# One encoder layer on one core: an earlier start and another order for the steps of the DeltaNet heads, and eight gate units instead of four at the border of two stages

## The chip, the cores and the metric

The kernel runs on one core of one Trainium2 chip. The metric is the device time of the program in microseconds (us). A core has TensorE (PE, with its weight loads as PEld), VectorE (DVE), ScalarE (ACT), GpSimd (POOL) and SyncE (SP), which here issues all DMA transfers from one queue.

## The reference

The layer takes 1024 tokens of width 1024 with 16 learned tokens ahead of them, all in float32. What matters of it:

```
h = rmsnorm(x)
q, k, v, z, b, a, sc_b, sc_c, sc_x, gate_a, gate_b = split(h @ w_in)
o   = gated_deltanet_bidir(q, k, v, z, b, a)      # 8 heads of 128, chunked, forward + backward
y_a = o @ w_branch_dn
y_b = (sc_b * depthwise_conv3(sc_c * sc_x)) @ w_branch_sc
x  += (sigmoid(gate_a) * y_a + sigmoid(gate_b) * y_b) @ w_out
x  += (silu(g) * u) @ w_down                       # g, u = split(rmsnorm(x) @ w_gate_up)
out = rmsnorm(x)[16:]

# one head, one direction, chunk by chunk (S: 128 x 128 state)
v_new = u_c - w_c @ S                              # u, w: solved from a unit triangular matrix
o_c   = (q_c * exp(g)) @ S + qk_c @ v_new
S     = S * exp(g_last) + k_dec_c.T @ v_new
```

q, k and v go through a centred convolution of five taps and SiLU first; q and k are normalised to unit length.

## The kernel before

**Matmuls.** A dense product of float32 is made of three: both operands are split into a high and a low part (a cast on ScalarE, a subtraction on VectorE, `split`, `split_part`), and high*high, high*low and low*high are added up in PSUM.

**The heads' stage.** The projection through w_in is cut into units of 128 output columns: 24 for q, k, v (`u_qkv`), 8 for z (`u_z`), 24 for the short convolution (`u_short`) and 16 for the merge gates (`u_gate`). A unit is two or three row blocks of 24 matmuls each (`dense_steps`, L290). The q, k, v units are taken when `qkv_ok` allows; all others are filling work, in the order z, short convolution, gates. The last LATE = 4 gates are kept back for later.

Beside them run, head by head, four generators: `g_decay` loads a mask-and-decay tile PQ (1 MB, broadcast) and takes its exponential; `g_norm` turns keys and queries with TensorE, squares and sums them, keeps the turned keys in the tile `kn` (two buffers) and multiplies keys and queries chunk by chunk into NP and PQ; `g_inv` inverts the triangular matrices; `g_scan` turns and scales the values (tile `vS`, one buffer) and then walks through eight chunks of 128 tokens from both ends, with four groups of small float32 matmuls per step (L742 and L745, L757, L774, L780) and VectorE and ScalarE between them. After the last step the outputs are normalised, scaled, turned (L83) and multiplied with z, which `g_scan` loads into the tile of the turned keys (L778).

**The inverse.** `g_inv` turns the 32 x 32 diagonal blocks of NP and stores them to DRAM (L591), loads them back as rows (L605), and solves them by substitution on VectorE: 31 pairs of a multiplication and a subtraction (`fs_job`, L446 and L450), each needing the one before. The result goes through DRAM again (L623, L628), and four rounds of small matmuls (L658 to L689) put the blocks together. The inverse's matmuls and the whole of the scan exclude each other through `lock["scan"]`.

**The order of the work** is written by a planner while the program is built. It keeps a model time for each engine (T) and emits a chain's next part when the model says that its inputs are ready; each engine then executes what it was given strictly in that order. VectorE's jobs wait in three lanes, "conv" (the convolutions, L313), "fs" (the substitution) and "norm"; `pump` takes from the ready lane that has spent least, weighted, so a convolution step fills the time in which a substitution step waits for its predecessor (DEP = 127 ns). A row buffer that is needed for a new projection forces the job that still holds it. Four streams hold at most one head each; the norm of head h starts when h < done + 2, where done counts finished scans, the scan when its head is inverted, and a head's projections are picked when h < done + 3. After a unit is picked its weights are loaded, and two units are ahead.

**The border.** After the stage its pools are closed, and the four late gate units follow (`dense`, L119 to L121; weights by `wload`, L104), while the first blocks of the next stage, a product of seven instead of eight block multiplications (`seven`, L1316), are loaded and combined (`front`). Then come the output projection (L1479 to L1481), the gate-up product (L1539 to L1541) and the down product (L1680 to L1682).

Of the kernel before, what the change touches and what calls it, by code (L numbers as in the profile page):

```python
# [8 lines left out]
F32 = mybir.dt.float32  # L9
# [7 lines left out]
P = 128  # L17
# [8 lines left out]
NC = 8  # L26
FF = 2816
NF = FF // P
LATE = 4
EPS = 1e-6  # L30
NEG = -1e30

# [5 lines left out]
def encoder_layer(ctx: ExitStack, tc: tile.TileContext, x, meta, norm1_w, w_in,  # L38
# [16 lines left out]
    def uid(s):  # L55
        cnt["n"] += 1
        return f"{s}_{cnt['n']}"
# [171 lines left out]
    def A(n):  # L229
        return on("act", 144 + 0.834 * n)  # L230
# [37 lines left out]
    def pump():  # L268
        while T["dve"] <= T["pe"] + 700:
            now = max(T["dve"], T["pe"])  # L270
            cand = [k for k, q in lanes.items() if q and q[0].ready <= now + 20]
            if not cand and any(q and q[0].ready <= now + DEP + 20 for q in lanes.values()):
                T["dve"] = now + DEP
                continue
            if not cand:
                return
            k = min(cand, key=lambda q: spent[q])
            spent[k] += lanes[k][0].step() * WEIGHT[k]
            if lanes[k][0].done:
                lanes[k].pop(0)  # L280
# [44 lines left out]
    def u_qkv(h, i, w):  # L325

        st_ = heads[h]
        if i == 0:
            st_["kq"] = d1.tile([P, 2, L], F32, tag="kq", name=uid("kq"), bufs=3)
            st_["vT"] = d1.tile([P, L], F32, tag="vT", name=uid("vT"), bufs=2)  # L330
        col = (8 + h, h, 16 + h)[i]
        dst = (st_["kq"][:, 0], st_["kq"][:, 1], st_["vT"])[i]
        raw = None
        sub = {"rows": 0}
        for ci, (t0, n) in enumerate(QUERY if i == 1 else QCH):
            po = psm()
            yield from dense_steps(po, w, hx, t0, n, sweep=(h == i == ci == 0))
            if raw is None:
                raw = row_buffer()
                if i != 1:  # L340
                    nc.gpsimd.memset(raw[:, 0:2], 0.0)
                nc.gpsimd.memset(raw[:, L + 2:L + 4], 0.0)
            nc.scalar.copy(raw[:, 2 + t0:2 + t0 + n], po[:, :n])
            nc.scalar.activation(dst[:, t0:t0 + n], po[:, :n], AF.Copy, scale=wc[:, 2, col:col + 1])  # L344
            A(n)
            A(n)
            sub["rows"] = 2 + t0 + n if ci < 2 else L + 4
            if ci == 1:
                job = enqueue("conv", conv_job(raw, dst, col, sub, META if i == 1 else 0))
                raws.append(job)  # L350
        key = ("tk", "tq", "tv")[i]

        def watch():
            return job.done
        st_[key] = watch
# [98 lines left out]
    def norm_job(st_, ssk1, cc, ce, he, y, sk):  # L454
        nc.vector.tensor_tensor(out=ce, in0=cc, in1=he, op=ALU.mult)
        V(18)
        yield T["dve"] + DEP
        nc.vector.tensor_tensor(out=sk, in0=y, in1=ssk1, op=ALU.mult)
        V(9)

    lock = {"scan": None}

# [5 lines left out]
    def g_decay(h, st_):  # L468

        st_["exp"] = {}  # L470
        PQ = st_["PQ"] = dn.tile([P, NC, 2, P], F32, tag="PQ", name=uid("PQ"), bufs=2)
        nc.sync.dma_start(PQ, grow[h:h + 1, 0:NC].broadcast_to([P, NC, 2, P]))
        yield T["pe"] + ARRIVE
        for c2 in range(NC // 2):
            pair = PQ[:, 2 * c2:2 * c2 + 2]
            nc.vector.tensor_tensor(out=pair, in0=pair, in1=mask2.unsqueeze(1).broadcast_to([P, 2, 2, P]), op=ALU.add)
            yield V(512)
            for c in (2 * c2, 2 * c2 + 1):
                for d in range(2):
                    hd = d * 8 + h  # L480
                    nc.scalar.activation(PQ[:, c, d], PQ[:, c, d], AF.Exp, bias=negG2[:, c, hd:hd + 1])
                    st_["exp"][c] = on("act", 295)
                yield T["act"]

    def g_norm(h, st_):

        kq = st_["kq"]
        kT, qT = kq[:, 0], kq[:, 1]
        small = dn.tile([P, 9, 12], F32, tag="small", name=uid("small"), bufs=2)
        st_["small"] = small  # L490
        ssk, ssq, rk2, ssk1, y, _, sk = (small[:, :, i] for i in range(7))
        cc, ce = small[:, :, 7:9], small[:, :, 9:11]
        nc.gpsimd.memset(small, 1.0)
        kn = dn.tile([P, 9, P], F32, tag="kn", name=uid("kn"), bufs=2)
        st_["kn"] = kn

        def square(src, dst, p=P):
# [40 lines left out]
                                  start=True, stop=True)  # L538
            return pk, pe(435)

        nxt = kkq(0)
        yield T["act"] + HOP
        nc.vector.tensor_scalar(out=ssk1, in0=ssk, scalar1=EPS, scalar2=None, op0=ALU.add)
        rsqrt(y, ssk1)
# [3 lines left out]
        nc.vector.tensor_tensor(out=cc, in0=hb, in1=rk2.unsqueeze(2).broadcast_to([P, 9, 2]), op=ALU.mult)  # L548
        nc.vector.tensor_scalar(out=Nm, in0=Nm, scalar1=cc[:META, 8, 0:1], scalar2=None, op0=ALU.mult)
        on("dve", 950)  # L550
        NP = dn.tile([P, NC, 2, P], F32, tag="NP", name=uid("NP"), bufs=2)
        PQ = st_["PQ"]
        st_["NP"] = NP
        yield T["act"] + HOP - 300
        for c in range(NC):
            pk, t = nxt
            if c + 1 < NC:
                nxt = kkq(c + 1)
            while c not in st_["exp"]:
# [12 lines left out]

    def g_inv(h, st_):
# [4 lines left out]

        nd = dr.tile([4, NC, 2, 32, 32], F32, tag="nd", name=uid("nd"), bufs=2)
        ndm = dr.tile([META, META], F32, tag="ndm", name=uid("ndm"), bufs=2)  # L580
        fN = dn.tile([P, 32, 32], F32, tag="fN", name=uid("fN"))
        fP = dn.tile([P, 16, 32], F32, tag="fP", name=uid("fP"))
        fPf = fP.rearrange("p j i -> p (j i)")
        mN = dn.tile([P, NC, 32], F32, tag="T2", name=uid("mN")).rearrange("p c i -> p (c i)")[:1]
# [3 lines left out]
        for b in range(4):  # L588
            nc.vector.transpose(NP[B(b), :, 1, B(b)], NP[B(b), :, 1, B(b)])
            on("dve", 467)  # L590
            nc.sync.dma_start(nd[b].rearrange("c d j i -> j (c d) i"),  # L591
                                             NP[B(b), :, :, B(b)].rearrange("j c d i -> j (c d) i"))
            if b < 3:
                yield T["dve"] - 200
        nc.gpsimd.memset(fP, 0.0)
        nc.gpsimd.memset(fPf[0:64, 0:8 * 33:33], 1.0)
        nc.gpsimd.memset(fPf[0:64, 8 * 32 + 24:512:33], 1.0)
# [32 lines left out]
        nc.sync.dma_start(Pm[:META, :META], pdm)  # L630

        Xe = dn.tile([P, NC, 32], F32, tag="Xe", name=uid("Xe"))
        XT = dn.tile([P, 2, 512], F32, tag="XT", name=uid("XT"))
        X64 = XT[:, 0].rearrange("p (c i) -> p c i", c=NC)
        nc.gpsimd.memset(X64[0:32, :, 32:64], 0.0)
        nc.gpsimd.memset(X64[96:128, :, 0:32], 0.0)
# [58 lines left out]
        lock["scan"] = None  # L695

    def g_scan(h, st_):
        nonlocal freed
        kq, vT, small, kn, NP, PQ, Pm = (st_[k] for k in ("kq", "vT", "small", "kn", "NP", "PQ", "Pm"))
        kT, qT = kq[:, 0], kq[:, 1]  # L700
        ssk, ssq, rk2, ssk1, y, _, sk = (small[:, :, i] for i in range(7))
        cc, ce = small[:, :, 7:9], small[:, :, 9:11]
# [7 lines left out]
        for grp in ((8, 0, 7), (1, 2, 3), (4, 5, 6)):  # L710
# [4 lines left out]
            for i, c in enumerate(grp):  # L715
                nc.scalar.activation(vS[:, c], pt[:, i], AF.Copy, scale=sk[:, c:c + 1])
                A(P)
        yield T["act"] + HOP - 1000

        oacc = [NP[:, c, c // 4] for c in range(NC)]  # L720

# [14 lines left out]
        for i in range(NC):  # L736
            cd = (i, NC - 1 - i)
            hd = (h, 8 + h)
            act_ = [d for d in range(2) if S[d] is not None]
            b1, b2 = newbank(), newbank()  # L740
            for d in act_:
                mm(b1[:, d], kT[:, cs(cd[d])], S[d], start=True, stop=True)  # L742
# [6 lines left out]
            for d in act_:  # L749
# [3 lines left out]
                                               op0=ALU.mult, op1=ALU.add)  # L753
                t = V(P, 1)
            yield t
            for d in range(2):
                mm(b1[:, 2 + d], NP[:, cd[d], d], r0[d], start=True, stop=True)  # L757
            yield pe(430)
# [13 lines left out]
            if i < NC - 1:  # L772
                for d in range(2):
                    mm(b1[:, d], kn[:, cd[d]], w[d], start=True, stop=True)  # L774
                t = pe(430)
            if i == NC - 2:
                zT = kn[:, 0:NC]
                nc.sync.dma_start(zT, z_d[h].rearrange("p (c t) -> p c t", c=NC))  # L778
            for d in range(2):
                mm(b2[:, 2 + d], PQ[:, cd[d], d], v2[d], start=True, stop=True)  # L780
            t2 = pe(430)
# [74 lines left out]
    fill_units += [(off + j * P, lambda w, j=j, i=i: u_short(j, i, w), None, i)  # L856
                   for j in range(8) for i, off in enumerate((OSC, OSX, OSB))]
    gates = [(j, off, d_[j]) for off, d_ in ((OGB, tb_d), (OGA, ta_d)) for j in range(8)]
    late = gates[len(gates) - LATE:]
    fill_units += [(off + j * P, lambda w, j=j, d_=d_: u_gate(j, d_, w), None, None) for j, off, d_ in gates[:len(gates) - LATE]]  # L860
    done = freed = 0
    decs, norms, invs, scans = [], [], [], []

    def qkv_ok():
        h, i = qkv_units[0][2:]
        return h < done + 3 and (i < 2 or h < nscan + 2)

    def pick():

# [21 lines left out]
    def start_streams():  # L891
# [3 lines left out]
            decs.append([g_decay(h, heads[h]), T["dve"] + HOP, h])  # L895
            ndec += 1
        h = nnorm
        if h < H and h < ndec and h < done + 2 and not norms and all(k in heads[h] and heads[h][k]() for k in ("tk", "tq")):
            norms.append([g_norm(h, heads[h]), T["dve"] + HOP, h])
            nnorm += 1  # L900
        h = ninv
# [1 line left out]
            invs.append([g_inv(h, heads[h]), T["dve"] + HOP, h])  # L903
            ninv += 1
        h = nscan
        if h < H and not scans and heads[h].get("inverted") and "tv" in heads[h] and heads[h]["tv"]():
            scans.append([g_scan(h, heads[h]), T["dve"] + HOP, h])
            nscan += 1

# [850 lines left out]
```

## Time and profile before

| | |
|---|---|
| median of 3 runs | 1994.02 us (1991.82 to 1994.43) |
| profiled execution | 1993.23 us, span 1991.5 us |
| granted TensorE clock | 0.995 of full, mean |
| instructions | 31817, of them 11977 matmuls |
| busy share | PE 99%, PEld 86%, DVE 71%, ACT 43%, POOL 8% |
| HBM | 184.34 MB read, 68.25 MB written |

The profile is one execution. An engine's line gives the sum of the times in which it was busy. A matmul's length in the records overlaps the next one's; its pace is read from start to start. A stretch's row gives for each engine its busy time and, in brackets, the number of its instructions, then the granted clock, the mean share of the 16 DMA engines and the GB/s. A row of waits gives the waiting engine, line and tile, what it waited for, the total in us, how often, and the longest. A row of the order of time gives start and length in us. "PEld" waiting is TensorE's queue standing before a weight load, which may still lie under a running matmul.

### The profile page before, as it was taken

Reading aid. Unit: us, or ns where it says so; the run is one execution under the profiler, and the core shown is the slowest. Engines: PE = TensorE matmul, PEld = TensorE weight load, DVE = VectorE, ACT = ScalarE, POOL = GpSimd, SP = SyncE. Lnnn points to the kernel's source line nnn. Section 1 sums busy time; section 2 is a strip of 40 time slices with the busy share of each in tenths; the row PEclk is TensorE's granted clock in tenths of the full one; section 3 lists DMA queues with packets and bytes.
Section 4 is the critical chain, followed back from the end, with each engine's and each line's share of the span. In section 5 each row is a group of like instructions: output and inputs, shape, how many; then the busy total and the mean of one; then the engine's idle time right before and its main releaser. Section 6 shows DMA issues by size and latency. Waiting matters only on the chain.

```text
span 1991.5 us, 31817 instructions
## 1 busy us (share of the span) xinstructions
PE 1962.7 (99%) x11977; PEld 1716.6 (86%) x11977; DVE 1406.2 (71%) x2744; ACT 846.6 (43%) x1984; POOL 165.8 (8%) x455
## 2 busy tenths in 40 slices
PE   8899999999999999999999999999999999999998
PEld 8898899999999999988888888787888888888887
DVE  4787476887779697866334888558987777856575
ACT  5364336555536464453442555224322322324343
POOL 3002011212020111201000000000000000000001
PEclk9999999999999999999999999999999999999999
DMA  4124322232322322233327732332765445487654
GB/s 143 42 63 117 104 62 80 65 96 49 96 59 81 75 75 70 65 84 83 106 78 276 259 110 87 111 117 90 262 229 180 157 146 184 156 278 247 194 171 169
DMA packets 245263, 254.66 MB, mean 128 GB/s; under 512 B 46644, under 2 KB 174949, under 8 KB 242677
## 3 DMA queue, kind: packets, MB, share of 16 engines
q1 hardware_dynamic: 245109, 252.63, 40.5%
q8 instruction: 94, 1.54, 0.3%
q14 instruction: 60, 0.49, 0.1%
HBM read 184.34 MB, written 68.25 MB: 127 GB/s over the span
## 4 chain that ended last, share of the span: by engine, by line
PE 92%; DVE 5%; ACT 2%; issue 1%; DMA 1%; SPq 0%; POOLq 0%; POOL 0%; DVEq 0%; ACTq 0%
PE pm L290 37%; PE pd L1541 3%; PE pd L1539 3%; PE pd L1540 3%; PE pm L1539 3%; PE pm L1540 3%; PE pm L1541 3%; PE pd L1316 2%; PE pm L1316 2%; PE pe L1541 2%; PE pe L1539 2%; PE pe L1540 2%; PE pd L757 2%; PE pe L537 1%; PE pe L1316 1%; PE pd L774 1%
## 5 line engine op out<-in xcount | busy, mean ns | idle before, releaser
L290 PE MATMUL pm<-hTh,wh 128*128 128x384 f32 (+4 forms) x1408 | 519.8, 370 | 2.9 <-ACT wh L888 2.8
L290 PE MATMUL pm<-hTh,wl 128*128 128x384 f32 (+4 forms) x1408 | 484.0, 345 | 1.1 <-DVE XT L674 0.9
L290 PE MATMUL pm<-al,wh 128*128 128x384 f32 (+4 forms) x1408 | 482.4, 343 | 0.5 <-DVE al L988 0.5
L290 PEld LDWEIGHTS pm<-hTh,wh 128*128 128x128 f32 x1408 | 266.8, 190 | 20.1 <-ACT wh L888 3.5
L290 PEld LDWEIGHTS pm<-hTh,wl 128*128 128x128 f32 x1408 | 265.4, 189 | 19.8 <-DVE wl L885 0.7
L290 PEld LDWEIGHTS pm<-al,wh 128*128 128x128 f32 x1408 | 266.9, 190 | 15.2 <-DVE al L988 0.7
L87 DVE TENSOR_TENSOR al<-raw,ring_h 128x1024 fp32r<-128x1024 f32 x73 | 88.1, 1222 | 64.5 <-ACT ring_h L86 64.0
L885 DVE TENSOR_TENSOR wl<-raw,wh 128x512 fp32r<-128x512 f32 x132 | 89.4, 689 | 59.0 <-ACT wh L888 58.3
L86 ACT CAST ring_h<-raw 128x1024 fp32r<-128x1024 f32 x73 | 76.5, 1053 | 104.4 <-PE pe L1682 36.2
L313 DVE SCALAR_TENSOR_TENSOR kq<-ra,wc,kq 128x520 f32<-128x520 f32 (+1 forms) x128 | 96.2, 752 | 9.7 <-ACT kq L344 6.6
L764 ACT ACTIVATE w<-pd,small 128x128 f32<-128x128 f32 x128 | 40.0, 364 | 110.6 <-PE pd L757 94.0
L128 POOL TENSOR_SCALAR ss<-ss 128x1 f32<-128x1 f32 x12 | 4.1, 343 | 903.1 <-ACT b L1692 607.8
L888 ACT CAST wh<-raw 128x512 fp32r<-128x512 f32 x132 | 77.0, 617 | 0.1
L450 DVE TENSOR_TENSOR fP<-fP,tm 128x135 f32<-128x135 f32 (+23 forms) x248 | 71.5, 288 | 5.2
L446 DVE TENSOR_TENSOR tm<-fP,fN 128x135 f32<-128x135 f32 (+23 forms) x248 | 71.7, 289 | 4.7
L789 DVE SCALAR_TENSOR_TENSOR S<-S,eGl,pd 128x128 f32<-128x128 f32 x104 | 31.8, 343 | 54.9 <-PE pd L774 26.8
L130 POOL TENSOR_TENSOR small<-small,minus_half 128x9 f32<-128x9 f32 x16 | 29.3, 1832 | 441.0 <-DVE small L824 309.9
L1277 DVE TENSOR_TENSOR b<-pm,b 128x512 f32<-128x512 f32 x65 | 43.6, 685 | 28.9 <-PE pm L1541 26.3
L613 POOL TENSOR_TENSOR tm<-mP,mN 1x15 f32<-1x15 f32 (+7 forms) x120 | 41.7, 347 | 228.4 <-DMA mN<-ndm 219.9
L1277 DVE TENSOR_TENSOR b<-pd,b 128x512 f32<-128x512 f32 x57 | 38.5, 685 | 24.8 <-PE pd L1541 24.7
L86 ACT CAST wh<-raw 128x1024 fp32r<-128x1024 f32 x28 | 29.5, 1053 | 56.7 <-issue 18.5
L313 DVE SCALAR_TENSOR_TENSOR vT<-ra,wc,vT 128x520 f32<-128x520 f32 x64 | 48.2, 753 | 6.4 <-ACT vT L344 5.4
(621 smaller groups left out, 4764.6 us busy)
## 6 DMA issues: line engine op xcount, KB each, us to landing
raw<-in_w_in_dram SPq DMA_DIRECT2D x72, 512.0 KB
raw<-in_w_gate_up_dram SPq DMA_DIRECT2D x44, 512.0 KB
sums<-in_w_down_dram SPq DMA_DIRECT2D x22, 512.0 KB
t_d<-sums SPq DMA_DIRECT2D x11, 1024.0 KB
raw<-s_d SPq DMA_DIRECT2D x44, 256.0 KB
raw<-t_d SPq DMA_DIRECT2D x44, 256.0 KB
act_d<-b SPq DMA_DIRECT2D x43, 256.0 KB
raw<-act_d SPq DMA_DIRECT2D x33, 256.0 KB
```

The source lines that it names most:

```text
L86: nc.scalar.copy(hi, src)
L87: nc.vector.tensor_tensor(out=lo, in0=src, in1=hi.bitcast(F32), op=ALU.subtract)
L290: mm(po[:, :n], (wl if j == 2 else wh)[:, k], xl[k][:, t0:t0 + n] if j == 1 else xh[k][:, t0:t0 + n], start=(i == 0), stop=(i == 3 * KT - 1))
L313: nc.vector.scalar_tensor_tensor(out=acc, in0=raw[:, h0 + t:h0 + t + hn], scalar=wc[:, t, col:col + 1], in1=acc, op0=ALU.mult, op1=ALU.add)
L446: nc.vector.tensor_tensor(out=tv, in0=fP[:, 0:r, j:j + 1].broadcast_to([P, r, n]), in1=fN[:, j:j + 1, j + 1:32].broadcast_to([P, r, n]), o ...
L885: nc.vector.tensor_tensor(out=u[1][1][:, k], in0=u[2][:, k], in1=u[1][0][:, k].bitcast(F32), op=ALU.subtract)
L888: nc.scalar.copy(u[1][0][:, k], u[2][:, k])
L1277: add = lambda out, a, b: nc.vector.tensor_tensor(out=out, in0=a, in1=b, op=ALU.add)
L1316: mm(bank[t], a[:, c], b[:, hi], start=fresh, stop=first and k == 3 and j == 2, skip_group_check=not first)
L1539: mm(po, ah[:, k], bhk, start=k == 0, stop=False)
L1540: mm(po, ah[:, k], blk, start=False, stop=False)
L1541: mm(po, al[:, k], bhk, start=False, stop=k == 3)
```

## The change

- LATE goes from 4 to 8: all eight gates of the DeltaNet branch are made at the border.
- `pump` takes "norm" and "fs" before "conv", and lets VectorE's model time wait for the next substitution step when that is ready within DEP.
- A third buffer of `kn`, four of `small`: the norm of head h may start when h < freed + 3 and any decay has started (freed counts scans whose last products are emitted), and waits ahead of its key products until done >= h - 1 and PQ is there.
- PQ is loaded in four parts, used 4, 6, 8 and 10 us after the request instead of all at 10.
- The scan starts as soon as its norm is finished and its values are convolved: it turns them, gives the lock back, waits for the inverse and takes the lock again. z is loaded into the tile of the turned values, in the last step instead of the one before it.
- Projections of q, k, v are picked when h < near + 3, where near counts scans that have reached their sixth step; `u_qkv` waits for freed >= h - 2.
- The inverse stores its four blocks without pauses between them; its tiles fN and XT share a buffer.

```
-LATE = 4
+LATE = 8
...
+            fs = lanes["fs"]
+            if fs and now + 20 < fs[0].ready <= now + DEP + 20:
+                T["dve"] = now = fs[0].ready
             cand = [k for k, q in lanes.items() if q and q[0].ready <= now + 20]
+            cand = [k for k in ("norm", "fs") if k in cand][:1] or cand
...
         if i == 0:
+            while freed < h - 2:
+                T["pe"] += 100
+                yield
...
-        nc.sync.dma_start(PQ, grow[h:h + 1, 0:NC].broadcast_to([P, NC, 2, P]))
-        yield T["pe"] + ARRIVE
         for c2 in range(NC // 2):
+            nc.sync.dma_start(PQ[:, 2 * c2:2 * c2 + 2], grow[h:h + 1, 2 * c2:2 * c2 + 2].broadcast_to([P, 2, 2, P]))
+        asked = T["pe"]
+        for c2 in range(NC // 2):
+            yield asked + 4000 + 2000 * c2
...
-        kn = dn.tile([P, 9, P], F32, tag="kn", name=uid("kn"), bufs=2)
+        kn = dn.tile([P, 9, P], F32, tag="kn", name=uid("kn"), bufs=3)
...
-        nxt = kkq(0)
...
+        while done < h - 1 or "PQ" not in st_:
+            yield T["pe"] + 100
...
+        nxt = kkq(0)
...
-            if b < 3:
-                yield T["dve"] - 200
...
-        XT = dn.tile([P, 2, 512], F32, tag="XT", name=uid("XT"))
+        XT = dn.tile([P, 2, 512], F32, tag="fN", name=uid("XT"))
...
+        lock["scan"] = None
         yield T["act"] + HOP - 1000
+        while not st_.get("inverted"):
+            yield T["pe"] + 100
+        yield from take("scan")
...
+            near += i == NEAR
...
+            if i == NC - 1:
+                zT = vS[:, 0:NC]
+                nc.sync.dma_start(zT, z_d[h].rearrange("p (c t) -> p c t", c=NC))
...
-            if i == NC - 2:
-                zT = kn[:, 0:NC]
-                nc.sync.dma_start(zT, z_d[h].rearrange("p (c t) -> p c t", c=NC))
...
-        return h < done + 3 and (i < 2 or h < nscan + 2)
+        return h < near + 3 and (i < 2 or h < nscan + 2)
...
-        if h < H and h < ndec and h < done + 2 and not norms and all(k in heads[h] and heads[h][k]() for k in ("tk", "tq")):
+        if h < H and ndec and h < freed + 3 and not norms and all(k in heads[h] and heads[h][k]() for k in ("tk", "tq")):
...
-        if h < H and not scans and heads[h].get("inverted") and "tv" in heads[h] and heads[h]["tv"]():
+        if h < H and not scans and heads[h].get("sk") and "tv" in heads[h] and heads[h]["tv"]():
```

More of the change, by code (lines that the diff above doesn't have):

```diff
@@ L459, in norm_job @@
         V(9)
+        st_["sk"] = True
     lock = {"scan": None}
@@ L488, in g_norm @@
         kT, qT = kq[:, 0], kq[:, 1]
-        small = dn.tile([P, 9, 12], F32, tag="small", name=uid("small"), bufs=2)
+        small = dn.tile([P, 9, 12], F32, tag="small", name=uid("small"), bufs=4)
         st_["small"] = small
@@ L580, in g_inv @@
         ndm = dr.tile([META, META], F32, tag="ndm", name=uid("ndm"), bufs=2)
-        fN = dn.tile([P, 32, 32], F32, tag="fN", name=uid("fN"))
+        fN = dn.tile([P, 2, 512], F32, tag="fN", name=uid("fN")).rearrange("p a (j i) -> p (a j) i", i=32)
         fP = dn.tile([P, 16, 32], F32, tag="fP", name=uid("fP"))
@@ L697, in g_scan @@
     def g_scan(h, st_):
-        nonlocal freed
-        kq, vT, small, kn, NP, PQ, Pm = (st_[k] for k in ("kq", "vT", "small", "kn", "NP", "PQ", "Pm"))
+        nonlocal freed, near
+        kq, vT, small, kn, NP, PQ = (st_[k] for k in ("kq", "vT", "small", "kn", "NP", "PQ"))
         kT, qT = kq[:, 0], kq[:, 1]
@@ L717, in g_scan @@
                 A(P)
+        lock["scan"] = None
         yield T["act"] + HOP - 1000
+        while not st_.get("inverted"):
+            yield T["pe"] + 100
+        yield from take("scan")
+        Pm = st_["Pm"]
         oacc = [NP[:, c, c // 4] for c in range(NC)]
@@ L858, in encoder_layer @@
     gates = [(j, off, d_[j]) for off, d_ in ((OGB, tb_d), (OGA, ta_d)) for j in range(8)]
-    late = gates[len(gates) - LATE:]
+    late = gates[max(0, len(gates) - LATE):]
     fill_units += [(off + j * P, lambda w, j=j, d_=d_: u_gate(j, d_, w), None, None) for j, off, d_ in gates[:len(gates) - LATE]]
-    done = freed = 0
+    NEAR = 5
+    done = freed = near = 0
     decs, norms, invs, scans = [], [], [], []
```

## The prediction

> **What bounds the kernel now.** I read the page first, then busy time by stretch, the waits of TensorE, the order of time around one head and around the border, and the groups of VectorE inside one head's substitution. The page:
>
> ```profile
> span 1991.5 us, 31817 instructions
> PE 1962.7 (99%) x11977; PEld 1716.6 (86%) x11977; DVE 1406.2 (71%) x2744; ACT 846.6 (43%) x1984; POOL 165.8 (8%) x455
> PE   8899999999999999999999999999999999999998
> PEclk9999999999999999999999999999999999999999
> ```
>
> TensorE is busy in every slice, all but 28.8 us of the span. The profiled execution took 1993.2 us, 1.7 more than its span; the median of the runs shown is 1994.0, 0.8 above it. The sum below goes against the 1993.2. Busy time by stretch (columns: PE, PEld, DVE, ACT, POOL, clock, DMA share, GB/s) shows where the 28.8 us lie:
>
> ```profile
> 0.00:50.00 50.00, 44.32 (x305) 41.69 (x306) 22.60 (x37) 26.27 (x54) 18.27 (x46) 1.00 0.47 143
> 50.00:101.00 51.00, 46.00 (x264) 43.22 (x263) 37.49 (x75) 19.50 (x46) 1.79 (x9) 0.90 0.16 42
> 101.00:1053.00 952.00, 948.16 (x7323) 868.89 (x7323) 672.85 (x1783) 464.54 (x1467) 130.46 (x368) 1.00 0.29 80
> 1053.00:1096.00 43.00, 43.00 (x191) 35.60 (x190) 23.33 (x20) 10.04 (x15) 0.00 (x0) 1.00 0.86 305
> 1096.00:1200.00 104.00, 104.00 (x460) 85.97 (x459) 88.87 (x96) 53.06 (x60) 0.00 (x0) 1.00 0.54 183
> 1200.00:1300.00 100.00, 96.13 (x431) 78.29 (x430) 66.74 (x86) 35.42 (x49) 2.40 (x6) 1.00 0.28 90
> ```
>
> The change touches the third row, the stage of the heads, and the fourth, the border with its four gate units. In the heads' stage TensorE is idle 952.00 - 948.16 = 3.8 us of 952; at the border not at all, nor in the hundred us behind it. The first 101 us, with 10.7 us idle, come before the first head has a substitution or a norm, so the planner emits them as before. What is idle after 1200 us belongs to the output projection and later, which the edits do not touch.
>
> That a busy PE is at its pace here, and not merely occupied, is seen in the order of time at the border (start, length):
>
> ```profile
> 1051.21 0.60 PE L83 MATMUL pd<-ident,NP 128*128 128x128 f32 x4
> 1051.56 0.47 PE L290 MATMUL pm<-hTh,wh 128*128 128x512 f32 x1
> 1051.88 0.39 PE L290 MATMUL pm<-al,wh 128*128 128x512 f32 x1
> 1052.10 0.39 PE L290 MATMUL pm<-hTh,wl 128*128 128x512 f32 x1
> 1052.33 0.40 PE L119 MATMUL pm<-hTh,wh 128*128 128x512 f32 x1
> ```
>
> Consecutive 512-column matmuls start 0.22 to 0.23 us apart, on both sides of the border; the fourth row of the stretches says the same (43.00 / 191 = 0.225). Two more things stand here. The last transposes of the last head (L83) come 1 us before the last projection of the stage (L290): chain and filling work now end together. And a gate unit has the same price inside the stage as behind it.
>
> **Gates, four to eight.** A gate unit is 2 x 24 matmuls of 512 columns. Four units are 192 x 0.225 = 43.2 us; they leave the stage and arrive at the border. Net 0: the heads' stage should end near 1053 - 43 = 1010, and the border last 86 us. Their weight loads move with them, each still one of 512 KB on SP, their casts become two long ones, and ScalarE and VectorE are far from full at the border (10.0 and 23.3 us of 43). The loads of the next stage already run there at a DMA share of 0.86 without any wait of TensorE; twice the time makes that easier, not worth more, since there is no wait to remove. I take 0; the bounds are the idle time of the fourth row, none, and a third of a us for each cast that comes late, so 0 to +1.5.
>
> **Substitution first.** The window of head 2's substitution, by groups of VectorE (busy, mean ns), and its first and last instruction:
>
> ```profile
> L313 DVE SCALAR_TENSOR_TENSOR kq<-ra,wc,kq 128x520 f32<-128x520 f32 (+1 forms) x12 | 9.0, 746 | 0.6 <-ACT kq L344 0.4
> L450 DVE TENSOR_TENSOR fP<-fP,tm 128x135 f32<-128x135 f32 (+23 forms) x31 | 8.9, 286 | 0.5
> L313 DVE SCALAR_TENSOR_TENSOR vT<-ra,wc,vT 128x520 f32<-128x520 f32 x8 | 6.0, 746 | 0.0
> L885 DVE TENSOR_TENSOR wl<-raw,wh 128x512 fp32r<-128x512 f32 x8 | 5.5, 683 | 0.0
> L813 DVE TENSOR_TENSOR NP<-pd,NP 128x128 f32<-128x128 f32 x10 | 2.9, 291 | 0.9 <-ACT NP L807 0.6
> L752 DVE SCALAR_TENSOR_TENSOR r<-pd,negEG,vS 128x128 f32<-128x128 f32 x9 | 2.8, 344 | 0.2
> L810 DVE SCALAR_TENSOR_TENSOR NP<-pd,eG,NP 128x128 f32<-128x128 f32 x8 | 2.7, 343 | 0.0
> 368.83 0.18 DVE L446 TENSOR_TENSOR tm<-fP,fN 128x31 f32<-128x31 f32 x1
> 424.01 0.18 DVE L446 TENSOR_TENSOR tm<-fP,fN 128x16 f32<-128x16 f32 x1
> 424.23 0.19 DVE L450 TENSOR_TENSOR fP<-fP,tm 128x16 f32<-128x16 f32 x1
> ```
>
> 62 short dependent steps take 55.6 us. The last pair shows their own pace: 0.22 us from start to start for 0.18 of work, 0.04 over the length. At the mean of 286 ns that is 62 x 0.33 = 20 us. Of the rest, convolution (L313) is 15.0 us, and the edit puts it off; the splits and the scan's steps (5.5 + 2.9 + 2.8 + 2.7 = 13.9 us, a quarter of the window) are not in the lanes and stay between. With the smaller groups I let them fill a third of VectorE's time; then the substitution lasts 20 / 0.67 = 30 us: 25 us less for a head like this one. VectorE gets no more work, only another order, and the idle time that the planner holds for each step's result (its 0.127 us; 62 x 0.127 = 8 us a head, 63 beside the 672.85 of 952 that it is busy). Who may now be late is a convolution, and behind it the projection's row buffer; a planner step forces a waiting convolution through when its buffer is wanted, and TensorE has three banks, 24 x 0.225 = 5.4 us each, before it must stop. Taken at 0; bounds -2 to +4.
>
> **Keys, values, decay.** These shorten one head's path, not the work. How far apart two heads are now, on the SP queue (issues of the first transfer of each inverse, and of the mask's load):
>
> ```profile
> 354.36 3.04 SPq L591 DMA_DIRECT2D nd<-NP  x4
> 398.77 0.34 SPq L472 DMA_DIRECT2D PQ<-grow  x1
> 458.56 2.50 SPq L591 DMA_DIRECT2D nd<-NP  x4
> 508.17 0.34 SPq L778 DMA_DIRECT2D kn<-z_d  x1
> ```
>
> The inverse of head 3 starts 104.2 us after that of head 2. Taking 25 us from it leaves some 80; the values turned beside the inverse take two or three us more off the path, an earlier norm (third key buffer) and the decay in quarters a few us of waiting between heads. The inverse's four stores are emitted without the planner's pauses; SP stands over them for 3.04 us already (first row), with one weight load behind. The z load moves from the seventh step of the scan to the eighth and from the keys' tile to the values', so SP now waits for VectorE's last r instead of a matmul. Its reader and that r:
>
> ```profile
> L752 DVE SCALAR_TENSOR_TENSOR r<-pd,negEG,vS x10: 340/344/350, 485.5 to 510.4; 128x128 f32<-128x128 f32 x10
> 523.22 0.74 DVE L845 SCALAR_TENSOR_TENSOR NP<-pd,cols,kn 128x512 f32<-128x512 f32 x1
> 300.80:304.60 3.80, 3.80 (x25) 3.80 (x25) 3.29 (x11) 0.81 (x4) 0.55 (x1) 1.00 0.82 286
> ```
>
> Issued at about 510.8, it has 12.4 us until its reader; at the 286 GB/s with which the mask's 1 MB moves in the last row, 512 KB take 1.8 us. Hidden; the weight load queued behind it on SP has two units (22 us) of slack. If that cover were gone, VectorE would stand before r and TensorE with it. The mask itself is now four issues of 0.34 us, one more us of SP per head, and VectorE reads the first quarter 4 us after the request instead of 10. By that row a quarter moves in about 1 us, so it is there after 2 us, or 4 with a weight load ahead of it: cost 0 to 1 us a head, taken 0.1, together +1.
>
> **Waits that are added.** A head's projections may be picked from the sixth step of the scan three heads back, and then wait, with nothing emitted but the chains, until that scan's last products. In the r row ten r's, five steps, lie from 485.5 to 510.4: 24.9 / 4 = 6.2 us a step, so under three steps, 17 to 18 us. A picked unit starts two units, 21.6 us, later. Cost 0, with 4 us to spare; without that cover up to 6 us for five heads. The norm now stands before its key products until the scan two heads back is done (behind it only its own stream waits), and the scan between its values and the inverse, its lock returned. The turned values are written on ScalarE after the previous head's last read of the same tile as z; ScalarE's evictions queue behind that write, for at most the 0.74 us of L845.
>
> **What can be won.** Only waits of TensorE. Those of the heads' stage, weight loads included (us in total, times, longest):
>
> ```profile
> PEld pd L757 <- DVE r L752: 3.8, 10, 0.5
> PEld pd L666 <- issue: 3.4, 8, 1.3
> PEld pd L681 <- issue: 2.8, 8, 0.7
> PEld pd L688 <- issue: 2.3, 8, 0.4
> PEld pd L774 <- ACT v L769: 1.9, 10, 0.2
> ```
>
> Together 14.2 us, partly under running matmuls. The middle three come once per head and the inverse's matmuls remain, so I let them stand; the r wait comes from what is ahead of r in VectorE's queue, a 746 ns convolution step or a 683 ns split. With 286 ns substitution steps in the convolution's place I take 1 us off. Sum: 1993.2 + 0 + 0 + 1 - 1 = 1993.
>
> The Trainium skill ("Perfetto Trace Analysis", Identifying the Most-Contended Engine) says that matmul busy time is a bad measure of the room TensorE has left, and to use the busy share of weight loads; by that, 86% would leave 14%. That reading is a rival below; the starts 0.225 us apart are against it.
>
> **Rivals.** (a) Fewer waits: shorter steps ahead of r and inverses that meet fewer long convolution steps. For it: the r row is VectorE's doing. Price: the r row and two thirds of the other four, 5 to 10 us off, 1983 to 1988. 0.25.
>
> (b) TensorE has room after all and the chain is what holds the stage. Price: weight loads are idle 952.00 - 868.89 = 83 us there, so up to that much off, 1910. Against it, the pace at the border, where no head is running, is the same. 0.02. It is the page's rule as a mechanism; here the trace speaks against the rule.
>
> (c) Slower, by VectorE's first-in-first-out queue: the mask's quarter is asked for too early, or a forced convolution sits ahead of r, while a scan runs. The scan's r, and L757 behind it, stand for the difference. It decides when a quarter lands over 4 us after the planner's request, which a busy DMA (0.86 at the border, 0.29 in the stage) would do. Price: 8 heads x 0.7 to 1.5 us, 1999 to 2005. 0.17. A longer wait costs double: around the 5.0 us idle in the second stretch the clock was 0.90 of full, 51 x 0.10 = 5 us more. The Trainium skill ("TensorE: Matmul & The Clock Gate", Part 1) has the same: an idle window of about 3.4 us halves the clock until a busy one has passed; that row agrees.
>
> (d) Slower, because the edit does not shorten the chain: the stage has 43.2 us less filling work, so seven distances between heads must each lose 43.2 / 7 = 6.2 us. Below that TensorE runs dry at the end: +43 at the worst, 2036; at 3 us saved, 2015. Speaking for it: starved convolutions delay the next head's norm. Against: 25 us from the substitution alone. 0.06.
>
> **How the numbers follow.** A change under 0.2% (4 us) is what measurements of this kernel cannot tell from none; the three runs spread by 2.6 us. Forecast 0.50 at 1993, (a) and (b) 0.27 faster, (c) and (d) 0.23 slower. The range 1985 to 2004 holds the forecast, about two thirds of (a) and most of (c): 0.8.
>
> **What would show it.** Right: 11977 matmuls, the last L290 near 1010, the border's stretch 86 us without idle time, substitutions of 27 to 35 us, heads some 80 to 85 us apart, the last head's transposes 50 us or more before the last L290, and idle time of TensorE from 101 us to the border of 2 to 8 us. Wrong: a stretch of only L742 to L780 before the border (d); r or mask waits of VectorE over 1 us (c); matmul starts closer than 0.22 us (b); or a gap or lost clock at the border, which I price at nothing.

## The result and the profile after

| | before | changed |
|---|---|---|
| median | 1992.92 us (1988.46 to 1994.43, 4 runs) | 2040.53 us (2036.06 to 2042.11, 4 runs) |
| profiled execution | 1993.23 us, span 1991.5 us | 2042.11 us, span 2040.4 us |
| granted clock, mean | 0.995 | 0.986 |
| matmuls | 11977 | 11977 |

The ratio of the runs is 1.0239, 95% interval 1.0215 to 1.0264: 48 us slower. The forecast was no change, and the range ended at 2004. The page of the changed kernel, the lines that answer to those shown of before:

```profile
span 2040.4 us, 31860 instructions
PE 1979.9 (97%) x11977; PEld 1727.4 (85%) x11977; DVE 1420.2 (70%) x2740; ACT 847.1 (42%) x1980; POOL 163.0 (8%) x455
PE   8999999989999999899999999999999999999998
PEclk9999999999999999999999999999999999999999
```

The same matmuls, but some slices of PE in the first half have dropped to 8. Busy time by stretch (PE, PEld, DVE, ACT, POOL, clock, DMA share, GB/s) places the loss; the fourth row is the end of the heads' stage, the fifth the border with its eight gate units:

```profile
0.00:50.00 50.00, 43.07 (x288) 40.45 (x289) 24.86 (x37) 26.36 (x54) 18.77 (x46) 0.97 0.47 143
50.00:101.00 51.00, 46.08 (x272) 43.49 (x271) 35.76 (x73) 18.16 (x45) 1.80 (x9) 0.93 0.12 33
101.00:1010.00 909.00, 874.78 (x6917) 804.38 (x6916) 670.79 (x1755) 441.86 (x1415) 125.35 (x367) 0.98 0.26 73
1010.00:1056.00 46.00, 46.00 (x222) 38.51 (x221) 10.29 (x23) 14.46 (x38) 1.81 (x1) 1.00 0.42 126
1056.00:1143.00 87.00, 87.00 (x385) 72.01 (x384) 28.10 (x24) 19.25 (x26) 0.00 (x0) 1.00 0.57 195
```

The border lasts 87 us and has no idle time. But it begins at 1056 where 1010 was expected, and in the heads' stage TensorE is idle 909.00 - 874.78 = 34.2 us; before, in the whole stage, it was 952.00 - 948.16 = 3.8. Inside that stage, by hundreds:

```profile
300.00:400.00 100.00, 96.70 (x817) 89.94 (x816) 78.41 (x208) 53.55 (x174) 13.79 (x44) 0.98 0.28 77
400.00:500.00 100.00, 90.02 (x764) 84.53 (x764) 73.78 (x189) 45.90 (x142) 13.10 (x44) 0.97 0.21 55
500.00:600.00 100.00, 97.74 (x833) 92.50 (x831) 83.26 (x215) 54.50 (x179) 15.79 (x47) 1.00 0.26 72
600.00:700.00 100.00, 94.78 (x800) 89.08 (x799) 78.79 (x205) 50.48 (x156) 17.50 (x47) 0.97 0.25 67
700.00:800.00 100.00, 94.32 (x788) 88.27 (x788) 78.07 (x206) 52.00 (x167) 15.79 (x45) 0.97 0.27 72
800.00:900.00 100.00, 93.80 (x770) 86.64 (x769) 72.05 (x186) 43.30 (x148) 16.73 (x44) 0.97 0.25 70
```

Five of these six stretches lose over 3 us, and each of the five also loses clock: 0.02 + 4 x 0.03 of 100 us are about 14 us of full-speed time (the clock is given to 0.01). Idle time 34.2 - 3.8 = 30.4, clock 14: some 44 of the 48.9 us between the two spans. What TensorE waited for in that stage (in us, times, longest), and what VectorE waited for of transfers:

```profile
PE pm L294 <- DVE wl L902: 18.9, 8, 5.7
PE pe L547 <- DVE PQ L579: 6.0, 3, 3.1
PE pd L776 <- DVE r L768: 5.9, 9, 1.7
```

```profile
DVE NP L575 <- DMA o_d<-NP: 8.8, 4, 4.0
DVE PQ L486 <- DMA PQ<-grow: 6.7, 2, 4.1
```

The first row did not exist before: projections (L294) stand because the low part of their weights (wl) is not there. One such place in the order of time, TensorE first, then VectorE:

```profile
841.09 0.41 PE L294 MATMUL pm<-hTh,wh 128*128 128x322 f32 x1 [0.91 <-ACT wh L905]
841.35 0.31 PE L294 MATMUL pm<-al,wh 128*128 128x322 f32 x1
846.54 0.64 PE L294 MATMUL pm<-hTh,wl 128*128 128x322 f32 x1 [4.89 <-DVE wl L902]
```

```profile
836.93 2.35 DVE L317 SCALAR_TENSOR_TENSOR vT<-ra,wc,vT 128x520 f32<-128x520 f32 x3
839.98 0.70 DVE L325 SCALAR_TENSOR_TENSOR vT<-rb,vT 128x520 f32<-128x520 f32 x1 [0.71 <-ACT rb L322]
840.60 0.48 DVE L368 TENSOR_SCALAR rb<-ra,cols 128x512 f32<-128x512 f32 x1
841.12 1.54 DVE L373 SCALAR_TENSOR_TENSOR rb<-ra,cols,rb 128x512 f32<-128x512 f32 x2
842.58 0.48 DVE L368 TENSOR_SCALAR rb<-ra,cols 128x512 f32<-128x512 f32 x1
843.09 1.54 DVE L373 SCALAR_TENSOR_TENSOR rb<-ra,cols,rb 128x512 f32<-128x512 f32 x2
844.54 0.68 DVE L408 TENSOR_TENSOR rb<-pm,rb 128x512 f32<-128x512 f32 x1
845.14 0.74 DVE L861 SCALAR_TENSOR_TENSOR NP<-pd,cols,vS 128x512 f32<-128x512 f32 x1
845.80 1.28 DVE L902 TENSOR_TENSOR wl<-raw,wh 128x512 fp32r<-128x512 f32 x2
```

VectorE is working all the while, at convolutions: the rest of a value convolution (L317), then a whole short convolution (L368, L373) that the unit at hand needs and so forces through, then that unit's product (L408) and a head's product with z (L861). The split of the next unit's weights (L902) stands behind all of it. The next matmul takes 0.64 us instead of 0.31: the granted clock from 846 to 849 us is 0.50. Where the convolutions had gone is seen in a table of L317 alone (L313 before) over head 5's substitution and the 26 us behind it; first before, then changed:

```profile
698.50:751.60 53.10, 15.19 (x20) 1.00 0.24 70
```

```profile
677.50:719.00 41.50, 0.58 (x2) 1.00 0.21 64
719.00:745.00 26.00, 5.72 (x8) 0.87 0.28 71
```

Before, 20 convolution steps went in between the substitution's; now none but two ends of steps. Counted in the same way over all eight substitutions, it was 76 of the 192 convolution steps before and is 25 now. The clock lost in the last row is not the convolutions' doing, however. It follows a wait for the bank of the key products, and VectorE, which has to empty that bank, stood for the store of o:

```profile
730.92 0.61 DVE L575 SCALAR_TENSOR_TENSOR NP<-pe,small,PQ 128x128 f32<-128x128 f32 x2 [4.03 <-DMA o_d<-NP]
732.61 1.19 PE L547 MATMUL pe<-kq 128*128 128x256 f32 x2 [3.15 <-DVE PQ L579]
```

### The profile page after: what moved, and what is told of

Same layout as the page of the kernel before. It is cut to its first block, busy times and chain, and to the rows that moved or that the text cites. A ratio compares the mean times of both kernels' runs of the same rounds, so it can differ in the third digit from the quotient of the medians.

```text
span 2040.4 us, 31860 instructions
## 1 busy us (share of the span) xinstructions
PE 1979.9 (97%) x11977; PEld 1727.4 (85%) x11977; DVE 1420.2 (70%) x2740; ACT 847.1 (42%) x1980; POOL 163.0 (8%) x455
## 4 chain that ended last, share of the span: by engine, by line
PE 81%; DVE 11%; DMA 3%; ACT 2%; issue 1%; SPq 1%; DVEq 0%; POOLq 0%; POOL 0%; ACTq 0%
PE pm L294 26%; PE pd L1558 3%; PE pd L1556 3%; PE pd L1557 3%; PE pm L1558 2%; PE pm L1556 2%; PE pm L1557 2%; PE pm L1333 2%; PE pd L1333 2%; PE pe L1558 2%; PE pe L1557 2%; PE pe L1556 2%; PE pe L1333 2%; PE pd L776 1%; PE pm L1698 1%; PE pm L1699 1%
## 5 line engine op out<-in xcount | busy, mean ns | idle before, releaser
L294 PE MATMUL pm<-hTh,wh 128*128 128x320 f32 (+4 forms) x1344 | 496.2, 370 | 3.9 <-ACT wh L905 3.9
L294 PE MATMUL pm<-hTh,wl 128*128 128x320 f32 (+4 forms) x1344 | 463.3, 346 | 19.0 <-DVE wl L902 18.9
L294 PE MATMUL pm<-al,wh 128*128 128x320 f32 (+4 forms) x1344 | 461.1, 344 | 0.5 <-DVE al L1005 0.5
L294 PEld LDWEIGHTS pm<-hTh,wl 128*128 128x128 f32 x1344 | 256.3, 191 | 38.3 <-DVE wl L902 21.9
L294 PEld LDWEIGHTS pm<-hTh,wh 128*128 128x128 f32 x1344 | 257.4, 192 | 19.8 <-ACT wh L905 5.0
L294 PEld LDWEIGHTS pm<-al,wh 128*128 128x128 f32 x1344 | 257.3, 192 | 14.2 <-DVE al L1005 0.7
L902 DVE TENSOR_TENSOR wl<-raw,wh 128x512 fp32r<-128x512 f32 x124 | 83.8, 689 | 65.0 <-ACT wh L905 64.6
L317 DVE SCALAR_TENSOR_TENSOR kq<-ra,wc,kq 128x520 f32<-128x520 f32 (+1 forms) x128 | 96.3, 752 | 6.0 <-ACT kq L351 3.8
L87 DVE TENSOR_TENSOR wl<-raw,wh 128x1024 fp32r<-128x1024 f32 x32 | 39.0, 1219 | 43.4 <-ACT wh L86 43.4
L350 ACT COPY ra<-pm 128x320 f32<-128x320 f32 (+3 forms) x72 | 32.2, 447 | 69.6 <-PE pm L294 69.5
L491 ACT ACTIVATE PQ<-PQ,negG 128x128 f32<-128x128 f32 x128 | 43.1, 394 | 36.6 <-DVE PQ L486 34.6
```

The source lines that it names most:

```text
L87: nc.vector.tensor_tensor(out=lo, in0=src, in1=hi.bitcast(F32), op=ALU.subtract)
L294: mm(po[:, :n], (wl if j == 2 else wh)[:, k], xl[k][:, t0:t0 + n] if j == 1 else xh[k][:, t0:t0 + n], start=(i == 0), stop=(i == 3 * KT - 1))
L317: nc.vector.scalar_tensor_tensor(out=acc, in0=raw[:, h0 + t:h0 + t + hn], scalar=wc[:, t, col:col + 1], in1=acc, op0=ALU.mult, op1=ALU.add)
L902: nc.vector.tensor_tensor(out=u[1][1][:, k], in0=u[2][:, k], in1=u[1][0][:, k].bitcast(F32), op=ALU.subtract)
```

## The experiments

Theory 1: convolutions put off by the substitution are forced through in bursts, ahead of the weights' low parts. Theory 2, its rival: the earlier key products make VectorE stand for a transfer (the store of o out of the buffer NP that they write next, the rows above), with its whole queue behind it. Theory 3: eight gate units leave the stage too little filling work.

**e1: the changed kernel without the planner's two edits.**

```
-            fs = lanes["fs"]
-            if fs and now + 20 < fs[0].ready <= now + DEP + 20:
-                T["dve"] = now = fs[0].ready
...
-            cand = [k for k in ("norm", "fs") if k in cand][:1] or cand
```

> The changed kernel with the planner's lanes as before (no preference for norm and substitution, no held idle time); all else as changed. Theory 1, starved convolutions: with the substitution first, convolution steps pile up and are forced through in one burst ahead of the low part of the next unit's weights (wl), TensorE stands and then runs at half clock; without the preference 1990 to 2000 us, idle time of TensorE from 101 us to the border under 10 us instead of 34. Theory 2, blocked queue: the earlier key products make VectorE stand for the store of o and for the mask's load, with everything behind it; then 2030 to 2042 here, since both stay. Theory 3, eight gate units: still 2035 to 2045.

**e2: the changed kernel with the norm's start as before.**

```
-        if h < H and ndec and h < freed + 3 and not norms ...
+        if h < H and h < ndec and h < done + 2 and not norms ...
```

> The changed kernel with the norm's start as before (own decay started and the scan two heads back finished); substitution still first. Theory 1: 2030 to 2042 us. Theory 2: the key products then come later than the store of o, VectorE no longer stands for it, 1993 to 2010. Theory 3: 2035 to 2045.

**e3: the kernel before with the planner's two edits alone** (the lines of e1, added).

> The kernel before with the two planner edits alone (norm and substitution first, held idle time for the next substitution step). Theory 1: slower than before by 20 to 45 us, with TensorE waits for wl of 10 us and more. Theory 2 and theory 3: as before within 4 us, since neither the early key products nor the gates are in it.

**e4: the changed kernel with LATE = 4.**

> The changed kernel with four gate units at the border, as before. Theory 1 and theory 2: 2036 to 2044 us, as changed, the waits lie in the middle of the stage. Theory 3, the filling work that the stage lost is what TensorE is missing: 1993 to 2000.

Measured: e1 2015.17 us, ratio to before 1.0105 (1.0075 to 1.0134); e2 2035.89, 1.0209 (1.0179 to 1.0238); e3 2025.43, 1.0156 (1.0127 to 1.0186); e4 2042.81, 1.0243 (1.0187 to 1.0299). Theory 3 falls with e4. The planner's edits cost a good half, alone (e3) and taken out (e1). In e3 TensorE waits 16.7 us for the parts of weights, but only 3.5 of it for wl; 13.2 are for the high part (wh), which ScalarE casts. One such place, ScalarE first, then TensorE:

```profile
404.81 0.64 ACT L322 ACTIVATE rb<-kq 128x520 f32<-128x520 f32 x1 [3.90 <-DVE kq L317]
407.27 1.12 ACT L892 CAST wh<-raw 128x512 fp32r<-128x512 f32 x2
407.93 0.64 PE L294 MATMUL pm<-hTh,wh 128*128 128x322 f32 x1 [4.32 <-ACT wh L892]
```

So a burst also works through ScalarE's queue: ScalarE stands with the tanh for VectorE's convolution, and the cast comes behind it. e2 stays within what theory 1 had for it; its largest waits are 12.2 us for wl and 9.1 for wh. But e1 is still 21 us over before, and not where theory 1 put it. Its longest rows, first of TensorE, then of VectorE's waits for transfers:

```profile
PE pe L543 <- DVE PQ L575: 12.7, 4, 4.3
```

```profile
DVE NP L571 <- DMA o_d<-NP: 12.7, 3, 5.2
```

No wait for wl is left. TensorE waits for the bank of the key products, and VectorE, which must empty it, for the store of o: theory 2. Both are true, so the next four cross them.

**e5: e1 and e2 together** (neither the preference nor the early norm).

> The changed kernel with both the lanes' preference and the early norm undone; eight gates, values turned beside the inverse, the mask in quarters and the earlier projections stay. Two causes (starved convolutions, and key products that meet the store of o): both are gone, 1992 to 1999 us, no wait of TensorE for wl or for the key products' bank over 1 us. If a third cause sits in what stays: over 2003.

**e6: e1, with the key products waiting for the store.** The second addition stands at the end of `g_scan`; LAND is 5500 ns of the planner's time.

```
-        while done < h - 1 or "PQ" not in st_:
+        while done < h - 1 or "PQ" not in st_ or (h > 1 and T["pe"] < heads[h - 2]["stored"]):
...
+        st_["stored"] = T["dve"] + LAND
```

> As e1 (no preference for the substitution), with the early norm kept, but the planner lets the first key products wait until 5.5 us after the last store of o two heads back was emitted. If the wait of VectorE for that store is the second cause: 1993 to 2000 us, and the 12.7 us in which VectorE stood for it are gone. If the early transposes and squares themselves cost the time: 2010 to 2016, as e1.

**e7: e2 without the hold** (the three lines of e1 that move the model time), preference kept; **e8: e2 without the preference** (the fourth line), hold kept.

> As e2 (late norm, 2036 us) with the preference for norm and substitution but without the held idle time. If the preference starves the convolutions: 2020 to 2036. If holding VectorE idle for the next step does it: 1993 to 2005, since between two steps a convolution step then goes in, as before.

> As e2 (late norm, 2036 us) with the held idle time but without the preference: the lanes take turns by time spent, as before. If the hold is what starves the convolutions: 2015 to 2036. If it is the preference: 1993 to 2005.

Measured: e5 2008.35 us, 1.0074 (1.0050 to 1.0098); e6 2001.13, 1.0037 (1.0021 to 1.0052); e7 2005.19, 1.0060 (1.0041 to 1.0080); e8 2039.46, 1.0233 (1.0204 to 1.0262). The preference is innocent: with the preference alone (e7) the kernel is as fast as without either (e5). The hold alone (e8) is as slow as both (e2). In the planner's terms: the gap of 0.127 us between two dependent steps used to be filled with a convolution step of 0.75 us, and that let 76 of them in; held shut, it lets in 25. And e6 settles theory 2: with the early transposes and squares kept and the store awaited, the 12.7 us are gone and TensorE's longest row is

```profile
PE pd L772 <- DVE r L764: 2.5, 5, 0.7
```

e5 came out over 2003, where it had put a third cause in what stays, and this one lies at the border:

```profile
1067.53 0.39 PE L121 MATMUL pm<-hTh,wl 128*128 128x512 f32 x1
1074.97 0.80 PE L119 MATMUL pe<-hTh,wh 128*128 128x512 f32 x1 [7.06 <-ACT wh L86]
```

```profile
1055.40 13.49 SPq L1375 DMA_DIRECT2D ta_d<-s  x5
1068.99 1.44 SPq L104 DMA_DIRECT2D raw<-in_w_in_dram  x2
```

A late gate stands for its weights; SP issued their load (L104) only at 1069, behind the stores of the gates before it (L1375), which went out over 13.5 us. Hence:

**e9: e6 with four gates. e10: the kernel before with eight gates and nothing else.**

> As e6 (no preference, no hold, key products after the store of o has landed) with four gate units at the border. If the eight units cost time by themselves, in TensorE's waits near the border: 1992 to 1998 us, 3 to 8 under e6. If e6's remaining 8 us come from the reordered chains in the middle of the stage: as e6, 1999 to 2003.

> The kernel before with eight gate units at the border and nothing else. Its chain is as long as before (last scan near 1050 us) while the filling work ends 43 us earlier. If the late gates can no longer fill the end of the chain: up to 43 us slower, 2010 to 2036. If TensorE runs late gates under the chain's end all the same: 1993 to 2005.

**e11: the changed kernel mended at both places; e12: the same with four gates.**

```
-            if fs and now + 20 < fs[0].ready <= now + DEP + 20:
+            if fs and not lanes["conv"] and now + 20 < fs[0].ready <= now + DEP + 20:
```

and the waiting for the store of e6.

> The changed kernel with two mends: VectorE's model time is held for the next substitution step only while no convolution job waits, and the key products wait for the store of o. Preference, early norm and eight gates stay. If hold and store are the two causes in the stage: 1995 to 2005 us, no wait for wl over 1 us. If the preference alone also starves convolutions: over 2010.

> As e11 with four gate units. If the eight units at the border are the third cause: 3 to 10 us under e11, 1992 to 1998, as before or slightly better. If not: as e11.

Measured: e9 1999.84 us, 1.0021 (1.0010 to 1.0032); e10 2003.32, 1.0034 (1.0020 to 1.0048); e11 2000.97, 1.0026 (1.0014 to 1.0038); e12 1995.19, 0.9992 (0.9982 to 1.0002). Eight gates cost 0.3% between e11 and e12 and on the kernel before (e10), about 7 us; between e6 and e9 the intervals overlap. e9 stays some 4 us over before, with 1 outside its interval; what those are is open. e10 also tells why it is 7 and not 43: TensorE's order mixes the late gates into the end of the chain.

```profile
995.04 0.47 PE L119 MATMUL pm<-hTh,wh 128*128 128x512 f32 x1
995.35 0.70 PE L742 MATMUL pd<-S,kq 128*128 128x128 f32 x4
1042.45 0.38 PE L83 MATMUL pd<-ident,NP 128*128 128x128 f32 x2
```

L119 is a late gate at 995, L742 a scan step, and the last head's transposes come 47 us later.

e11 shows the heads' stage mended, with preference, early norm and values beside the inverse all in place (busy time from 101 to 1010 us, and TensorE's longest wait there):

```profile
101.00:1010.00 909.00, 903.89 (x7115) 833.91 (x7115) 663.22 (x1764) 450.26 (x1432) 125.27 (x367) 1.00 0.29 78
```

```profile
PE pd L758 <- DVE S L805: 2.4, 1, 2.4
```

Idle 5.1 us instead of 34.2, the clock whole, 7115 matmuls in the stretch instead of 6917. Inside the eight substitutions there are 70 convolution steps again.

What was still open is how the hold does it: by the order in VectorE's queue, or because the held time is missing.

**e13: the changed kernel with the store awaited and the next unit's weights split earlier; e14: with the store awaited only; e15: e12 with the earlier splits; e16: the kernel before with them.**

```
-    SPL = (11, 12, 13, 14)
+    SPL = (3, 4, 5, 6)
```

> The changed kernel, hold and preference kept, key products after the store of o, and the next unit's weights split 3 to 6 matmul triples into a unit instead of 11 to 14, so ahead of the forced convolutions in VectorE's queue. If the order does it: 2000 to 2012 us and TensorE's waits for wl under 3 us. If the held idle time is missing as capacity: as e14, 2022 to 2036, the wait only moves to evictions or r.

> The changed kernel with the key products after the store of o, nothing else. The store cost some 14 us without the hold (e1 against e6); here the waits for wl stay: 2022 to 2036 us, TensorE's wait for the key products' bank under 1 us instead of 6.

> As e12 (hold only without waiting convolutions, key products after the store, four gates: 0.9992 of before) with the earlier splits. Few waits are left to remove: 1990 to 1996 us, within 4 us of before.

> The kernel before with the earlier splits alone. TensorE has no wait for wl there, only for r behind a split (3.8 us in all): 1989 to 1997 us, the same as before.

Measured: e13 2017.16 us, 1.0120 (1.0094 to 1.0146); e14 2032.17, 1.0195 (1.0170 to 1.0220); e15 1992.03, 0.9991 (0.9980 to 1.0002); e16 1991.66, 0.9991 (0.9980 to 1.0002). TensorE's longest rows, e14 first, then e13:

```profile
PE pm L294 <- DVE wl L903: 21.5, 6, 5.9
PE pd L776 <- DVE r L768: 4.1, 6, 1.4
```

```profile
PE pe L547 <- DVE PQ L579: 3.6, 3, 1.9
PE pd L676 <- ACT T L670: 3.3, 1, 3.3
PE pd L83 <- ACT NP L855: 3.3, 2, 1.6
```

With the splits ahead of the bursts the waits for wl are gone altogether, and a good 40% of what the hold costs comes back (1.0195 to 1.0120, of 1.0195 to 1.0026). Earlier splits do not do that by themselves (e16). The rest stays: TensorE now waits for the chain's own steps. Ahead of the longest of these waits stands a burst once more: ScalarE waits with the tanh for VectorE's convolution, and T, which TensorE needs, comes behind it.

```profile
419.78 0.64 ACT L322 ACTIVATE rb<-kq 128x520 f32<-128x520 f32 x1 [7.05 <-DVE kq L317]
422.09 0.21 PE L676 MATMUL pd<-NP,T 32*32 32x32 f32 x1 [3.33 <-ACT T L670]
```

But VectorE also stands 9.7 us there in four waits for the mask's load (6.7 in two in the changed kernel, none in e11), so a part may be the mask's. So e13 was between both expectations: order in the queue for a good 40%; for the rest it was not separated whether late convolutions, the held time itself or the mask are to blame. No version beats the kernel before by more than its measurement tells: e12, e15 and e16 all have 1 in their intervals.

Step by step, then, each run one mend further than the one ahead of it: changed 1.0239; store awaited (e14) 1.0195; hold only without waiting convolutions (e11) 1.0026; four gates (e12) 0.9992. That is 9, 34 and 7 us (the intervals of the first two just overlap, so the 9 is the least certain). Taken out in another order the parts differ: the store alone is 14 us where there is no hold (e1 to e6), and eight gates show no loss where TensorE is late anyway (e4).

## Why the prediction was wrong

- **What bounds the kernel** was right: 11977 matmuls, the pace unchanged, nothing won (e12 has the whole chain rearranged and as many gates as before, and takes the same time). No run speaks for rival (b).
- **Substitution first** is the step that failed: "Who may now be late is a convolution ... Taken at 0; bounds -2 to +4." The prediction named the held 8 us per head, the late convolution and the forcing, and took three free banks in front of TensorE for cover. But the burst does not only hold up evictions. In VectorE's queue the next unit's wl stands behind it (in ScalarE's, wh: 13.2 us in e3), and these parts have no bank in front of them. Measured between e14 and e11, which differ in the hold alone, the step cost 34 us. The gain was mis-sized too: from first to last step the eight substitutions took 40.9 us in the mean, against 49.4 before, not 25 less; head 2's took 44.6. In e11, with convolutions let in again, it is 51 us: the shortening and the loss came and went together. And the heads did not come 80 to 85 us apart: from the first store of head 0's o to that of head 7's it is 307.40 to 1028.80, 103 us a head, against 105 before.
- **Keys**: the early norm was costed only as time off the path. That its key products write the buffer from which the store of o two heads back is still being read was not seen: the sum has no term for this part; it measured 9 us in the changed kernel, 14 without the hold. The row was there to be asked for: the NP writes of before came after the norm's front, 16 to 28 us behind that store; in the changed kernel they come 2 to 5 us behind its issue.
- **Gates**, "0 to +1.5": 87 us without idle time in the changed kernel, as forecast, but 7 us where the rest is in order (e10, e12). The load of a late gate behind stores on SP, 7.06 us in e5, was not counted. In e11 TensorE waits for a late gate's weights for 2.1 us only; where the rest of its 7 us lies was not separated.
- **Mask in quarters**: the wait was named and priced at 0 to 1 us a head; VectorE stood 6.7 us in two of them, while e11 has none. After the first, 4.14 us until 303.82, ScalarE stands for VectorE's step on the mask (4.15 us, L491), and TensorE, for ScalarE's next step (L855), 1.41 us until 306.23. e14 has one such wait of VectorE, 4.1 us, so its price lies within the 34 us between e14 and e11.
- **Rivals.** (c) had the direction and the right machine, VectorE's queue with a forced convolution in it, at 0.17 and at most a quarter of the price: it looked for the loss at r (5.9 us in the changed kernel) and not at wl (18.9). Its sentence that a longer wait costs double held in part: some 14 of the 48 us are clock, beside 30 of idle time, so about half as much again. The row that it gave as agreeing with a window of 3.4 us has no single wait of that length: the two longest in it are 2.76 us, until 55.65, and 2.03 us, until 95.15. (d) gave 2036, next to the measured time, for a reason that did not happen: the chain ended at 1031, 25 us before the filling work, and e10 shows that a long chain costs 7 us, not 43.
- The range came out too narrow because (c) was priced by what one transfer can be late, not by what a burst of queued work can.

## What to carry to other kernels

When one chain gets a queue first, ask what was living in its gaps, and what is queued behind that when it is finally forced; price the burst (its whole length, here 836.93 to 845.80, 8.9 us) and not the step, and include the work that has no buffer in front of it. A shorter path for a chain was worth nothing here while the engine that bounds the kernel was full, and it moved the chain's buffers into transfers that used to be over. Look up, for each tile written earlier, the last transfer that reads it. And a gap of a few us on TensorE can be paid a second time, at half clock.

## What the runs showed of the hardware

A gap can cost more than its length. After the 4.89 us wait shown above the matmul of 322 columns took 0.64 us instead of 0.31, and in the heads' stage of the changed kernel every stretch of 100 us that lost over 3 us to waits also shows a granted clock of 0.97 or 0.98, where before all of them show 1.00. The Trainium skill ("TensorE: Matmul & The Clock Gate", Part 1) has the clock halved after an idle window of about 3.4 us; that wait agrees. The length of one wait does not decide it here, though, and the measurement decides over that rule: after 1.41 us until 306.23 and 3.15 us until 732.61 the clock from 308 to 310 and from 734 to 736 is 0.54 and 0.50, while after 2.65 us until 411.83 it stays at 1.00 to 420.

And a store holds its source for longer than its own bytes take: in the changed kernel the second half of one head's o, 256 KB, was issued at 406.39 and VectorE's write into that buffer began at 410.62, 4.2 us later. At the 253 GB/s that all transfers together moved from 408 to 410 us, 256 KB are about 1.0 us (an estimate); other transfers were under way beside it.
